# One residual stream instead of two in a list-scheduled transformer kernel: pre-norm gains applied to the transposed stream

## The chip, the cores and the metric

One core of one Trainium2 chip. The metric is the device time of one execution in microseconds. The profile is one execution on the chip, taken by the hardware profiler. TensorE is PE in the rows (PEld its weight loads), VectorE is DVE, ScalarE is ACT, GpSimd is POOL, and SyncE, which issues the loads, is SP.

## What is computed

A decoder of two blocks of two layers each, on one sequence of 256 tokens, 1024 wide, in fp32. Every stage has the same frame: a root-mean-square norm with a pre-gain goes in, the stage's own work is done, and the result is normed with a post-gain and added to the residual stream `x`:

```python
def rms_norm(x, g):
    y = x * lax.rsqrt(jnp.mean(x * x, axis=-1, keepdims=True) + EPS)
    return y * g

for l in range(2):                       # first block
    y = swiglu(rms_norm(x, ffn1_pre_g[l]), ...);        x = x + 0.5 * rms_norm(y, ffn1_post_g[l])
    y = hybrid_mixer(rms_norm(x, mix_pre_g[l]), ...);   x = x + rms_norm(y, mix_post_g[l])
    y = memory_xattn(rms_norm(x, xa_pre_g[l]), ...);    x = x + rms_norm(y, xa_post_g[l])
    y = swiglu(rms_norm(x, ffn2_pre_g[l]), ...);        x = x + 0.5 * rms_norm(y, ffn2_post_g[l])
for l in range(2):                       # second block
    h = rms_norm(x, g_pre_mix[l]);  mix = concat(pool_mixer, dsa_attention of h @ w_in[l]) @ w_out[l]
    x = x + rms_norm(mix, g_post_mix[l])
    h = rms_norm(x, g_pre_ffn[l]);  f = square(relu(h @ w_ff1[l])) @ w_ff2[l]
    x = x + rms_norm(f, g_post_ffn[l])
```

That makes twelve stages: feed-forward, mix, cross-attention, feed-forward, twice over; then mix2 and relu2, twice over. Between them lie eleven hand-overs, each for two row tiles.

## The kernel before

**Tiles.** The 256 tokens are two row tiles `t` = 0, 1 of 128 rows. Tokens lie along the partitions in `x[t]` (128x1024; `x_4` and `x_5` in the order, `x` in the trace). Every fp32 operand of the large products is split into a high part, rounded to fp32r, and the rest, and `mm3` (L518) makes one product of three matmuls: low by high, high by low, high by high. A projection needs the stream with its 1024 features along the partitions: `xT[t]`, a pair of 128x8x128 tiles (high and low), eight slices of 128 features. `xmm` (L523) goes through the eight slices, three matmuls each. Weights come by DMA into `raw`, and `split` (L492) makes `wH` (a copy on ACT) and `wL` (a subtraction on DVE).

**The norm.** The scale `rstd` of a row is left out of the transposed stream and applied when a finished projection is taken out of PSUM, as `scale=rstd[t]` of an ACT instruction (`m<-mm,sm`, `s<-mm,sm`, `nat<-mm,sm` in the trace). `rms_scale` (L531) makes it from a sum of squares: a small DVE instruction, then a power on POOL. The sum of squares of `x` is one ACT instruction, `junkx<-x`.

**The hand-over.** Two streams are kept: `x`, and `xg` = `x` times the next stage's pre-gain. `prepare` (L628) runs earlier in the stage: it broadcasts the post-gain `gp` and the next pre-gain `gg` to 128 partitions, makes `xg[t] = x[t]*gg` and `gg = gg*gp`. `boundary` (L642) runs when the stage's result `acc` (two PSUM tiles of 512 columns for a row tile) is finished:

1. `rms_two` (L544) makes the scale `r` of the post-norm: a sum of squares of each `acc` half on ACT (`junk<-acc`), and a power on POOL.
2. `yg = acc*gg` and `xg += yg*r` on DVE, a half at a time.
3. `transpose_in` (L558) transposes `xg` on PE, four 128x128 transposes into one PSUM tile `tr` (of which there are two), and splits each `tr` with one 512 wide copy on ACT and one 512 wide subtraction on DVE into `xT`.
4. Marked as background: `yp = acc*r` on ACT (`m<-acc,sm`), `yp *= gp` and `x += yp` on DVE, a half at a time.
5. `rstd[t]` of the next stage from the sum of squares of `x[t]`.

**At the start** `start_stream` (L592) loads the first pre-gain as 8x128, transposes it on PE to `gT` (128x8, so that a partition holds its features' gains), and `begin` multiplies the transposed `x` by it, 512 columns in one DVE instruction, before the split.

**What sets the order.** Nothing is issued where it is written. `Recorder.add` (L220) records each operation with the operations it depends on; `plan` (L430) is a list scheduler with a modelled cost for each instruction: PE and SP keep the order of the program, the other engines take what is ready by a deadline (background work yields), and the best of six passes is emitted. So each engine has one fixed order of instructions, and all of them carry the line of `emit`, L449. Two rules of the recorder matter: engines that touch the same PSUM tile are ordered against each other even if both only read (the term `b.psum and o.eng != eng` in `add`), and SP may run 250 PE operations ahead. Buffers (L474): eight `m2` of 512 columns, thirteen `m4` of 1024, four `xT`, and in PSUM four `acc`, two `mm`, two `tr`.

## Time and profile before

| what | value |
|---|---|
| three runs | median 1919.25 us (1919.09 to 1920.76) |
| the profiled execution | 1919.18 us, its span 1917.3 us |
| PE busy | 1886.3 us, 98% of the span |
| DVE busy | 1289.2 us, 67% |
| ACT busy | 1064.1 us, 55% |
| POOL busy | 67.6 us, 4% |
| DMA | 337.55 MB, 176 GB/s |

The span is the time between the first and the last instruction of the profile. A busy share is the time in which an engine executed something, over the span. In a timeline the number in brackets is the time that the engine stood idle before the instruction, and the name behind the arrow is what released it. Buffer numbers are left out of the names: `m` stands for all `m2` and `m4` tiles, `sm` for small columns of one or two numbers (`r` and `rstd` among them), `s` and `nat` for working tiles.

The hand-overs lie here (us from the start of the span): feed-forward to mix at 199 to 210 and 847 to 858; mix to cross-attention at 375 to 381 and 1024 to 1030; cross-attention to feed-forward at 460 to 467 and 1110 to 1117; feed-forward to feed-forward, between the layers, at 652 to 676; feed-forward to mix2 at 1302 to 1320; mix2 to relu2 at 1417 to 1437 and 1720 to 1740; relu2 to mix2 at 1604 to 1622.

### The profile page before, as it was taken

The page shows a single profiled execution, that of the slowest core. Times are in us where ns is not written, and L with a number is a line of the kernel's source. Part 1 is how long each engine was busy: PE and PEld are TensorE (multiplying, and loading weights), DVE is VectorE, ACT ScalarE, POOL GpSimd, SP SyncE. Part 2 cuts the span into 40 slices and gives each one's busy share as a digit, 9 for nine tenths or more (in the row PEclk, how much of TensorE's full clock was granted, in tenths as well). Part 3 has the DMA queues.
Part 4 walks back from the last instruction along what each step waited for, and adds up shares of the span by engine and source line. Part 5 has one row for each costly group of instructions (what it writes and reads, how often), then busy time and mean ns, then how long its engine had stood idle before and what let it go on. Part 6 is the DMA issues. An engine that isn't in the chain of part 4 may idle for free.

```text
span 1917.3 us, 25346 instructions
## 1 busy us (share of the span) xinstructions
PE 1886.3 (98%) x9109; PEld 1536.7 (80%) x9109; DVE 1289.2 (67%) x2172; ACT 1064.1 (55%) x1721; POOL 67.6 (4%) x82
## 2 busy tenths in 40 slices
PE   9999999999999999999999999999999999999998
PEld 7888788888788778878788878888778888777887
DVE  6555888866654764568978675558976557976554
ACT  5444776556444644467656554447664446565443
POOL 0000100100000000010010000000000000000000
PEclk9999999999999999999999999999999999999999
DMA  8555654554655565648354465555446555535553
GB/s 265 179 184 181 202 174 138 176 176 154 202 180 190 164 199 187 194 142 262 113 192 149 144 211 178 184 165 185 141 136 216 186 178 160 176 121 195 178 176 110
DMA packets 230958, 337.55 MB, mean 176 GB/s; under 512 B 17768, under 2 KB 123696, under 8 KB 230832
## 3 DMA queue, kind: packets, MB, share of 16 engines
q1 hardware_dynamic: 230832, 335.92, 54.6%
q8 instruction: 72, 1.18, 0.2%
q14 instruction: 54, 0.44, 0.1%
HBM read 334.82 MB, written 1.05 MB: 175 GB/s over the span
## 4 chain that ended last, share of the span: by engine, by line
PE 81%; DVE 7%; ACT 4%; DMA 3%; issue 3%; POOL 1%; SPq 0%; DVEq 0%; POOLq 0%; ACTq 0%
PE mm L449 46%; PE acc L449 30%; PE tr L449 5%; DVE m L449 2%; ACT wH L449 2%; DVE wL L449 1%; POOL sm L449 1%; ACT m L449 1%; DMA raw<-in_xa_wk_dram 1%; DVE x L449 1%; DMA raw<-in_ffn_w_up_dram 1%; DVE xT L449 1%; DVE xg L449 1%; DMA m<-in_ffn_pre_g_dram 0%; DVE sm L449 0%
## 5 line engine op out<-in xcount | busy, mean ns | idle before, releaser
L449 DVE TENSOR_TENSOR wL<-raw,wH 128x1024 fp32r<-128x1024 f32 (+3 forms) x612 | 731.1, 1200 | 294.2 <-ACT wH L449 285.5
L449 PE MATMUL mm<-wH,xT 128*128 128x512 f32 (+2 forms) x2880 | 912.9, 391 | 7.5 <-ACT m L449 3.7
L449 ACT ACTIVATE wH<-raw 128x1024 fp32r<-128x1024 f32 (+3 forms) x612 | 634.6, 1040 | 313.4 <-PE mm L449 151.3
L449 PEld LDWEIGHTS mm<-wH,xT 128*128 128x128 f32 x2880 | 535.8, 188 | 124.3 <-ACT m L449 4.6
L449 PE MATMUL mm<-wL,xT 128*128 128x512 f32 (+2 forms) x1440 | 565.2, 393 | 0.5 <-DVE wL L449 0.5
L449 PE MATMUL acc<-wH,m 128*128 128x512 f32 (+1 forms) x1408 | 452.1, 393 | 0.5 <-DVE m L449 0.5
L449 PEld LDWEIGHTS mm<-wL,xT 128*128 128x128 f32 x1440 | 271.1, 188 | 56.2 <-DVE wL L449 2.5
L449 PEld LDWEIGHTS acc<-wH,m 128*128 128x128 f32 (+1 forms) x1408 | 258.1, 186 | 55.9 <-DVE m L449 1.3
L449 PE MATMUL acc<-wL,m 128*128 128x512 f32 (+1 forms) x736 | 281.5, 386 | 0.0
L449 PEld LDWEIGHTS acc<-wL,m 128*128 128x128 f32 (+1 forms) x736 | 134.9, 183 | 29.0
L449 ACT ACTIVATE s<-mm,sm 128x256 f32<-128x256 f32 x88 | 41.7, 474 | 188.3 <-PE mm L449 179.8
L449 DVE SCALAR_TENSOR_TENSOR s<-mm,sm,s 128x256 f32<-128x256 f32 x88 | 42.3, 481 | 137.9 <-ACT s L449 137.9
L449 ACT ACTIVATE m<-tr 128x256 fp32r<-128x256 f32 (+5 forms) x208 | 87.6, 426 | 58.7 <-PE tr L449 51.1
L449 POOL TENSOR_TENSOR sm<-sm,neghalf 128x1 f32<-128x1 f32 (+1 forms) x60 | 53.6, 894 | 1842.6 <-ACT sm L449 1665.3
L449 DVE TENSOR_TENSOR m<-tr,m 128x256 fp32r<-128x256 f32 (+3 forms) x192 | 93.1, 495 | 7.3 <-ACT m L449 5.7
L449 PE MATMUL mm<-wH,m 128*128 128x512 f32 x256 | 89.2, 409 | 0.0
L449 PE MATMUL acc<-wH,xT 128*128 128x512 f32 x256 | 82.4, 398 | 0.0
L449 DVE TENSOR_TENSOR m<-acc,m 128x512 f32<-128x512 f32 (+1 forms) x64 | 39.6, 621 | 60.3 <-ACT junk L449 59.4
L449 ACT ACTIVATE nat<-mm,sm 128x512 f32<-128x512 f32 x56 | 38.5, 687 | 70.9 <-PE mm L449 63.4
L449 ACT ACTIVATE junk<-acc 128x512 bf16<-128x512 f32 x48 | 28.5, 593 | 67.9 <-PE acc L449 67.7
L449 PEld LDWEIGHTS acc<-wH,xT 128*128 128x128 f32 x256 | 48.2, 188 | 10.5
L449 ACT ACTIVATE sc<-sc,sm 128x128 f32<-128x128 f32 (+1 forms) x96 | 42.8, 447 | 22.7 <-DVE sm L449 22.0
(152 smaller groups left out, 1469.6 us busy)
## 6 DMA issues: line engine op xcount, KB each, us to landing
raw<-in_w_ff_dram SPq DMA_DIRECT2D x128, 512.0 KB, 4.2
raw<-in_ffn_w_gate_dram SPq DMA_DIRECT2D x176, 256.0 KB, 3.3
raw<-in_ffn_w_up_dram SPq DMA_DIRECT2D x176, 256.0 KB, 3.8
raw<-in_ffn_w_down_dram SPq DMA_DIRECT2D x88, 512.0 KB, 5.0
raw<-in_w_in_dram SPq DMA_DIRECT2D x80, 512.0 KB, 3.8
raw<-in_w_out_dram SPq DMA_DIRECT2D x32, 512.0 KB, 4.1
raw<-in_cmp_w_dram SPq DMA_DIRECT2D x16, 512.0 KB, 4.7
raw<-in_xa_wk_dram SPq DMA_DIRECT2D x16, 512.0 KB, 5.3
```

The source lines that it names most:

```text
L449: getattr(getattr(self.nc, op.eng), op.name)(*[r(v) for v in op.args], **{k: r(v) for k, v in op.kw.items()})
```

## The change

The stream `xg` goes. `prepare` loads the next pre-gain as eight rows of 128 (`load_gT`, 4 KB) and PE transposes it to `gT` (`turn_gT`); the post-gain is scaled by `c` only where `c` is not 1. `boundary` makes `yp = acc*gp` and `x += yp*r` directly, a half at a time, transposes `x`, and the gain is applied as `tr` is split: `transpose_in` with `gT` goes through the four 128 wide pieces of a `tr`, and for each one ACT makes `xh = tr*gT` with the gain as a scale by partition, and DVE makes `tr*gT - xh`. Where a row tile had two copies and two subtractions 512 wide, it now has eight and eight 128 wide. The background part is gone, and `rstd[t]` comes from `x[t]` as before. `begin` uses the same code.

```diff
--- before.py
+++ after.py
@@ -555,7 +555,20 @@
 
         return Lazy(lambda t: (T("xT", [128, 8, 128], F32R), T("xT", [128, 8, 128], F32R)))
 
-    def transpose_in(xt, src, k0=0, nk=8):
+    def load_gT(vec):
+
+        g8 = T("g8", [8, 128], bufs=2)
+        SP.dma_start(g8, vec.rearrange("(k p) -> k p", p=128))
+        return g8
+
+    def turn_gT(g8):
+        tr = P("tr")
+        PE.transpose(tr[:, :8], g8, ident[:8, :8])
+        gT = T("gT", [128, 8], bufs=2)
+        DVE.tensor_copy(gT, tr[:, :8])
+        return gT
+
+    def transpose_in(xt, src, k0=0, nk=8, gT=None):
 
         for b in range(0, nk, 4):
             m = min(4, nk - b)
@@ -563,11 +576,17 @@
             for k in range(m):
                 PE.transpose(tr[:, k * 128:k * 128 + 128], src[:, (b + k) * 128:(b + k) * 128 + 128], ident)
             ks = slice(k0 + b, k0 + b + m)
+            if gT is not None:
+                for k in range(m):
+                    xh, v, g = xt[0][:, k0 + b + k, :], tr[:, k * 128:k * 128 + 128], gT[:, b + k:b + k + 1]
+                    ACT.activation(xh, v, AF.Copy, scale=g)
+                    DVE.scalar_tensor_tensor(xt[1][:, k0 + b + k, :], v, g, xh.bitcast(F32),
+                                             op0=ALU.mult, op1=ALU.subtract)
+                continue
             split(xt[0][:, ks, :], xt[1][:, ks, :], tr[:, :m * 128].rearrange("p (k n) -> p k n", n=128))
 
 
     x = [T(f"x{t}", [128, D]) for t in range(2)]
-    xg = [T(f"xg{t}", [128, D]) for t in range(2)]
     xr = a["x"].rearrange("o (t p) d -> (o t) p d", p=128)
 
     def load_x(t, b):
@@ -591,15 +610,11 @@
 
     def start_stream(pre):
 
-        g8 = T("g8", [8, 128])
-        SP.dma_start(g8, pre.rearrange("(k p) -> k p", p=128))
+        g8 = load_gT(pre)
         SP.dma_start(ident, cst[:, _C_ID:_C_ID + 128])
         load_x(0, 0)
         ACT.activation(small(1), eps, AF.Silu)
-        tr = P("tr")
-        PE.transpose(tr[:, :8], g8, ident[:8, :8])
-        gT = T("gT", [128, 8])
-        DVE.tensor_copy(gT, tr[:, :8])
+        gT = turn_gT(g8)
         xT = new_xT()
         z = T("nat", [128, 128])
         DVE.memset(z, 0.0)
@@ -611,15 +626,7 @@
             for b in range(2):
                 if t or b:
                     load_x(t, b)
-                tr = P("tr")
-                for k in range(4):
-                    c = b * 512 + k * 128
-                    PE.transpose(tr[:, k * 128:k * 128 + 128], x[t][:, c:c + 128], ident)
-                ks = slice(b * 4, b * 4 + 4)
-                n = T("nat", [128, 4, 128])
-                DVE.tensor_tensor(n, tr.rearrange("p (k n) -> p k n", n=128),
-                                  gT[:, ks].unsqueeze(2).to_broadcast([128, 4, 128]), op=ALU.mult)
-                split(xT[t][0][:, ks, :], xT[t][1][:, ks, :], n)
+                transpose_in(xT[t], x[t][:, b * 512:b * 512 + 512], 4 * b, 4, gT[:, 4 * b:4 * b + 4])
             if t == 0:
                 for i in range(3):
                     PE.matmul(warm[:, :128], x[t][:, :128], z, start=True, stop=True)
@@ -629,46 +636,25 @@
 
         gp = T("m4", [128, D])
         bcast_load(gp, post)
-        DVE.tensor_scalar(gp, gp, c, None, op0=ALU.mult)
-        if pre_next is None:
-            return gp, None
-        gg = T("m4", [128, D])
-        bcast_load(gg, pre_next)
-        for t in range(2):
-            DVE.tensor_tensor(xg[t], x[t], gg, op=ALU.mult)
-        DVE.tensor_tensor(gg, gg, gp, op=ALU.mult)
-        return gp, gg
+        if c != 1.0:
+            DVE.tensor_scalar(gp, gp, c, None, op0=ALU.mult)
+        return gp, None if pre_next is None else turn_gT(load_gT(pre_next))
 
     def boundary(t, acc, gains, xT_next):
 
-        gp, gg = gains
-        last = gg is None
+        gp, gT = gains
         r = rms_two(acc[0], acc[1], 512, D)
-        if not last:
-            yg = T("m4", [128, D])
-            for h in range(2):
-                sl = slice(h * 512, h * 512 + 512)
-                DVE.tensor_tensor(yg[:, sl], acc[h], gg[:, sl], op=ALU.mult)
-                DVE.scalar_tensor_tensor(xg[t][:, sl], yg[:, sl], r, xg[t][:, sl], op0=ALU.mult, op1=ALU.add)
-            transpose_in(xT_next[t], xg[t])
-        yp = T("m4", [128, D])
-        halves = [slice(h * 512, h * 512 + 512) for h in range(2)]
-        if last:
-            for h, sl in enumerate(halves):
-                DVE.tensor_tensor(yp[:, sl], acc[h], gp[:, sl], op=ALU.mult)
-            for c in range(0, D, 512):
-                sl = slice(c, c + 512)
-                DVE.scalar_tensor_tensor(x[t][:, sl], yp[:, sl], r, x[t][:, sl], op0=ALU.mult, op1=ALU.add)
+        for h in range(2):
+            sl = slice(h * 512, h * 512 + 512)
+            yp = T("m2", [128, 512])
+            DVE.tensor_tensor(yp, acc[h], gp[:, sl], op=ALU.mult)
+            DVE.scalar_tensor_tensor(x[t][:, sl], yp, r, x[t][:, sl], op0=ALU.mult, op1=ALU.add)
+            if gT is None:
                 SP.dma_start(out.rearrange("o (t p) d -> (o t) p d", p=128)[t][:, sl], x[t][:, sl])
-            return
-        rec.background = True
-        for h, sl in enumerate(halves):
-            evict(yp[:, sl], acc[h], r)
-        for sl in halves:
-            DVE.tensor_tensor(yp[:, sl], yp[:, sl], gp[:, sl], op=ALU.mult)
-            DVE.tensor_tensor(x[t][:, sl], x[t][:, sl], yp[:, sl], op=ALU.add)
-        rec.background = False
-        rstd[t] = rms_scale(sumsq(x[t], D), D)
+            else:
+                transpose_in(xT_next[t], x[t][:, sl], 4 * h, 4, gT[:, 4 * h:4 * h + 4])
+        if gT is not None:
+            rstd[t] = rms_scale(sumsq(x[t], D), D)
 
 
     def ffn_like(nch, load_up, up, load_down, nk, gains, xT, xTn, begin=None):
```

The first place is DVE at the first hand-over from cross-attention to feed-forward (around 464 us in the trace of before). Before, `acc_4294` and `acc_4384` are row tile 1's result, `xg_7` and `x_5` its streams, `xg_6` and `x_4` those of row tile 0; `xT_4435` belongs to row tile 0:

```order
L449 TENSOR_TENSOR m_1022_4367<-acc_4294,m_961_4090 128x512
L449 TENSOR_TENSOR m_1005_4305<-acc_4343,m_961_4090 128x512
L449 SCALAR_TENSOR_TENSOR xg_6_321<-m_1005_4305,sm_4397,xg_6_321 128x512 x2
L449 TENSOR_TENSOR wL_4417<-raw_4325,wH_4400 128x1024
L449 TENSOR_TENSOR xT_4435<-tr_4415,xT_4425 128x512
L449 TENSOR_TENSOR xT_4435<-tr_4423,xT_4425 128x512
L449 TENSOR_TENSOR wL_4447<-raw_4338,wH_4413 128x1024
L449 TENSOR_TENSOR m_1022_4367<-acc_4384,m_961_4090 128x512
L449 SCALAR_TENSOR_TENSOR xg_7_354<-m_1022_4367,sm_4469,xg_7_354 128x512 x2
L449 TENSOR_TENSOR m_1010_4407<-m_1010_4407,m_960_4086 128x512 x2
L449 TENSOR_TENSOR x_4_78<-x_4_78,m_1010_4407 128x512 x2
```

Row tile 0's pieces, 512 wide, stand ahead of row tile 1's update of `xg_7`, and the update of the true `x_4` comes last. In the changed kernel, with `x_4` and `x_5` the streams, `tr_4453` and `tr_4463` the two transposed halves of row tile 0, and `sm_4515` the scale `r` of row tile 1:

```order
L449 SCALAR_TENSOR_TENSOR xT_4472<-tr_4453,gT_4246,xT_4461 128x128
L449 TENSOR_TENSOR wL_4477<-raw_4377,wH_4450 128x1024
L449 SCALAR_TENSOR_TENSOR xT_4472<-tr_4453,gT_4246,xT_4461 128x128
L449 SCALAR_TENSOR_TENSOR xT_4472<-tr_4463,gT_4246,xT_4461 128x128
L449 TENSOR_SCALAR sm_4495<-sm_4467 128x1
L449 TENSOR_TENSOR m_1026_4511<-acc_4423,m_958_4127 128x512
L449 SCALAR_TENSOR_TENSOR xT_4472<-tr_4453,gT_4246,xT_4461 128x128
L449 SCALAR_TENSOR_TENSOR x_5_117<-m_1022_4406,sm_4515,x_5_117 128x512
L449 SCALAR_TENSOR_TENSOR xT_4472<-tr_4453,gT_4246,xT_4461 128x128
L449 SCALAR_TENSOR_TENSOR xT_4472<-tr_4463,gT_4246,xT_4461 128x128
L449 SCALAR_TENSOR_TENSOR x_5_117<-m_1026_4511,sm_4515,x_5_117 128x512
L449 SCALAR_TENSOR_TENSOR xT_4472<-tr_4463,gT_4246,xT_4461 128x128
```

Four pieces of row tile 0 stand ahead of the first update of `x_5` and two more between the first and the second; `x_4` was updated before all of these.

The second place is ACT at the same hand-over. Before, `junk_4453` is the sum of squares of row tile 1's second half, `junkx_4511` that of `x` of row tile 0:

```order
L449 ACTIVATE junk_4453,sm_4454<-acc_4384 128x512
L449 ACTIVATE sm_4462<-sm_4454,sm_4363 128x1
L449 ACTIVATE wH_4466<-raw_4369 128x1024
L449 ACTIVATE m_1027_4476<-acc_4294,sm_4469 128x512
L449 ACTIVATE m_1027_4476<-acc_4384,sm_4469 128x512
L449 ACTIVATE xT_4491<-tr_4484 128x512
L449 ACTIVATE xT_4491<-tr_4494 128x512
L449 ACTIVATE junkx_4511,sm_4512<-x_4_78 128x1024
```

Now, with `junkx_4466` the sum of squares of row tile 0's `x` and `junk_4503` that of row tile 1's second half:

```order
L449 ACTIVATE xT_4461<-tr_4453,gT_4246 128x128
L449 ACTIVATE junkx_4466,sm_4467<-x_4_78 128x1024
L449 ACTIVATE xT_4461<-tr_4453,gT_4246 128x128
L449 ACTIVATE xT_4461<-tr_4463,gT_4246 128x128
L449 ACTIVATE wH_4486<-raw_4391 128x1024
L449 ACTIVATE junk_4503,sm_4504<-acc_4423 128x512
L449 ACTIVATE sm_4509<-sm_4504,sm_4402 128x1
L449 ACTIVATE xT_4461<-tr_4453,gT_4246 128x128
L449 ACTIVATE xT_4461<-tr_4463,gT_4246 128x128
L449 ACTIVATE xT_4461<-tr_4453,gT_4246 128x128
L449 ACTIVATE wH_4521<-raw_4408 128x1024
L449 ACTIVATE xT_4461<-tr_4463,gT_4246 128x128
```

The sum of squares of `x_4` has moved ahead of row tile 1's, and the copies of `tr` stand one by one between the weights' `wH`.

The third place is PE in the first feed-forward stage, where `g_145` is the pre-gain of the mix stage that follows:

```order
L449 MATMUL acc_440<-wH_517,m_101_522 128x512
L449 MATMUL acc_440<-wL_528,m_100_510 128x512
L449 MATMUL acc_440<-wH_517,m_100_510 128x512
L449 MATMUL tr_723<-ident_73,g_145_241 128x8
L449 MATMUL mm_725<-wH_665,xT_113 128x512
L449 MATMUL mm_725<-wL_673,xT_107 128x512
L449 MATMUL mm_725<-wH_665,xT_107 128x512
```

The transpose `tr_723` is new; it stands alone between matmuls 512 wide. Five of the eleven new transposes stand so, and six next to transposes or matmuls of 256 columns or fewer.

## Rows read from the trace of the kernel before

**Rows 1.** The page, part 1: busy time, share of the span, instructions.

```profile
PE 1886.3 (98%) x9109; PEld 1536.7 (80%) x9109; DVE 1289.2 (67%) x2172; ACT 1064.1 (55%) x1721; POOL 67.6 (4%) x82
```

**Rows 2.** Busy time by stretch: us, busy (count) per engine, PEclk, DMA share, GB/s.

```profile
720.00:780.00 60.00, 60.00 (x267) 48.46 (x266) 30.27 (x34) 26.14 (x33) 0.00 (x0) 1.00 0.60 193
...
1305.00:1315.00 10.00, 7.58 (x54) 6.84 (x53) 9.54 (x17) 7.47 (x15) 1.10 (x2) 1.00 0.31 89
...
sum 171.00, PE 159.21 PEld 129.59 DVE 146.04 ACT 113.89 POOL 31.69; mean PE 9.37 PEld 7.62 DVE 8.59 ACT 6.70 POOL 1.86
```

**Rows 3.** Timeline 203 to 211 and one PE row at 1309.94: start, duration [idle<-releaser].

```profile
204.03 1.28 DVE L449 TENSOR_TENSOR x<-x,m 128x512 f32<-128x512 f32 x2
...
205.34 1.06 ACT L449 ACTIVATE junkx<-x 128x1024 bf16<-128x1024 f32 x1 [0.65 <-DVE x L449]
...
207.31 2.19 POOL L449 TENSOR_TENSOR sm<-sm,neghalf 128x1 f32<-128x1 f32 x1 [2.80 <-DVE sm L449]
...
209.54 0.69 ACT L449 ACTIVATE m<-mm,sm 128x512 f32<-128x512 f32 x1 [0.46 <-POOL sm L449]
...
210.28 0.55 PE L449 MATMUL tr<-ident,m 128*128 128x128 f32 x3 [1.07 <-ACT m L449]
...
1309.94 1.29 PE L449 MATMUL tr<-ident,xg 128*128 128x128 f32 x8 [1.14 <-DVE xg L449]
```

**Rows 4.** Groups by line and form: busy us, mean ns, idle before.

```profile
L449 DVE TENSOR_TENSOR m<-m,m 128x512 f32<-128x512 f32 x48 | 31.4, 683 | 0.1
...
L449 ACT ACTIVATE m<-acc,sm 128x512 f32<-128x512 f32 x44 | 28.5, 675 | 0.1
...
L449 DVE TENSOR_TENSOR x<-x,m 128x512 f32<-128x512 f32 x44 | 28.2, 682 | 0.0
...
L449 DVE TENSOR_TENSOR xg<-x,m 128x1024 f32<-128x1024 f32 x22 | 26.3, 1216 | 1.0 <-DMA m<-in_ffn_pre_g_dram 1.0
```

**Rows 5.** Timeline 463 to 467, first hand-over from cross-attention to feed-forward.

```profile
463.64 0.39 PE L449 MATMUL mm<-wH,xT 128*128 128x512 f32 x1
...
463.84 0.60 ACT L449 ACTIVATE junk<-acc 128x512 bf16<-128x512 f32 x1
463.87 0.39 PE L449 MATMUL mm<-wL,xT 128*128 128x512 f32 x1
...
464.56 0.69 DVE L449 TENSOR_TENSOR m<-acc,m 128x512 f32<-128x512 f32 x1 [0.23 <-ACT junk L449]
...
464.93 0.55 POOL L449 TENSOR_TENSOR sm<-sm,neghalf 128x1 f32<-128x1 f32 x1 [5.83 <-ACT sm L449]
...
465.51 1.42 DVE L449 SCALAR_TENSOR_TENSOR xg<-m,sm,xg 128x512 f32<-128x512 f32 x2 [0.27 <-POOL sm L449]
```

**Rows 6.** Timeline of the start, PE.

```profile
17.71 0.50 PE L449 MATMUL mm<-wH,xT 128*128 128x512 f32 x1 [0.57 <-DVE xT L449]
```

**Rows 7.** Timeline 225 to 227, PE, around a lone narrow transpose.

```profile
225.14 0.40 PE L449 MATMUL mm<-wL,xT 128*128 128x512 f32 x1
225.46 0.23 PE L449 MATMUL tr<-ident,pe 16*128 16x16 f32 x1
225.62 0.73 PE L449 MATMUL mm<-wH,xT 128*128 128x512 f32 x2
226.19 0.40 PE L449 MATMUL mm<-wL,xT 128*128 128x512 f32 x1
```

**Rows 8.** Groups by line and form, the shapes nearest to the new pieces.

```profile
L449 ACT ACTIVATE m<-tr 64x128 fp32r<-64x128 f32 x32 | 8.0, 269 | 3.8 <-DVE m L449 3.6
...
L449 DVE SCALAR_TENSOR_TENSOR s<-sc,sm,s 128x128 f32<-128x128 f32 x14 | 4.9, 350 | 0.3
...
L449 ACT ACTIVATE nat<-mm,scl 128x256 f32<-128x256 f32 x8 | 3.6, 470 | 0.4 <-PE mm L449 0.4
```

**Rows 9.** Timeline 1305 to 1306, PE, blocks 292 wide.

```profile
1305.44 0.29 PE L449 MATMUL mm<-wH,xT 128*128 128x292 f32 x1
1305.57 0.29 PE L449 MATMUL mm<-wL,xT 128*128 128x292 f32 x1
```

## The prediction

> **What bounds the kernel now.** I read the page's busy times first, then busy time by stretches of the span, then the waits of TensorE in order of time, and last the costs by shape. TensorE (PE) is busy 98% of the span [rows 1]. In the long feed-forward stretches it is busy all the time, with VectorE (DVE) at half load (the stretch 720 to 780 in [rows 2]), so nothing that DVE or ScalarE (ACT) is spared there can shorten the program, and everything that PE is given there lengthens it. What is left to win lies where one stage hands over to the next. I laid 13 stretches around the handovers in which PE waited, and 4 around handovers in which it did not (mix to cross-attention, both layers): PE is busy 159.21 of 171.00 us in them (the sum in [rows 2]), so the handovers hold 11.8 us of idle PE. The worst is the one into the first mix2 stage, 2.4 us (1305 to 1315 in [rows 2]).
>
> What these waits are made of shows in the first one [rows 3]. The two additions into `x` (row tile 0) run on DVE until 205.31, its sum of squares follows on ACT, the power on POOL lasts from 207.31 to 209.50, and only then can ACT scale the finished projection by `rstd` (209.54); PE, which needs that result for its next transposes, has stood for 1.07 us. So the wait is for `rstd`, and `rstd` is late because the true `x` is updated in the background, after `xg`. Most of the others read alike (a scaled copy or a SiLU that waits for POOL); in the one into mix2 PE also waits 1.14 us for `xg` itself [rows 3].
>
> **The change part by part.** *Work taken off DVE and ACT.* Gone are 22 products `xg = x*gg`, 44 of the 48 products with `gp` in SBUF, 44 additions into `x` and 44 scaled copies on ACT: 26.3 + 28.8 + 28.2 us of DVE and 28.5 of ACT [rows 4]; the eleven `gg*gp` and eight scalings by 1.0 go too. I price all this at nothing by itself: PE covers it. It counts only through what it lets happen earlier.
>
> *`rstd` comes earlier.* In the new program `x` is complete right after the two updates that follow `r`, 1.42 us for the pair (the last of [rows 5]). Two products and two additions leave the chain to `rstd`, 2.7 us at 0.68 each [rows 4], with the scaled copies and all that stood between them, and in the new order the sum of squares of row tile 0 stands ahead of row tile 1's on ACT. No single wait is as long as that. I take all 11.8 us as freed (bounds 0 and 11.8). At the start, PE's 0.57 us wait for a whole split half [rows 6] goes as well, since the first piece now suffices: 0.6 us.
>
> *Eleven more transposes on PE.* Every `turn_gT` puts an 8x128 transpose into PE's queue. The nearest row is the lone transpose of `pe`, 16 partitions: from the matmul before it to the second start after it are 1.05 us, where three matmuls at 0.23 take 0.69, so it costs 0.36; its own slot is 0.16 [rows 5, 7]. In the new order five of the eleven stand alone between wide matmuls and six next to other narrow work, where I charge the slot only: 5 x 0.36 + 6 x 0.16 = 2.7 us, all of it on the bound (bounds 11 x 0.16 = 1.8 and 11 x 0.36 = 3.9). Its load is 4 KB in place of 512 KB on SP's queue, and stands at least 50 PE rows, over 10 us, before the transpose: nothing.
>
> *The split into eight pieces.* This is the part that costs. Before, a half of the transposed tile (512 wide) was one copy on ACT and one subtraction on DVE. Now each 128 wide piece is a scaled copy on ACT and a subtraction on DVE. They read the same PSUM tile, and the program lets two engines read one PSUM tile only in turn: before, DVE's product with `acc` already waited for ACT's sum of squares of the same `acc` (464.56 in [rows 5]). So within a tile ACT's piece 2 waits for DVE's piece 1. A lap is one ACT piece, one DVE piece and two hand-overs. No row has the ACT piece: 128 wide without a pointer takes 0.27, 256 wide with one 0.47 [rows 8]; I take 0.36, the middle. DVE's piece, the same instruction at the same width with its source in SBUF, is 0.35 [rows 8]; I take that. A hand-over is 0.05 (ACT ends at 210.23, PE starts at 210.28 [rows 3]). Lap: 0.81 us. PE eats a piece in three matmuls: 0.70 us where the stage's blocks are 512 wide [rows 5], 0.40 where they are 292 wide [rows 9]. At the nine handovers of the first kind a tile of four pieces falls behind by four times 0.11, so 0.4 us each, 3.6 in all. At the two into mix2 the pieces of the two tiles alternate, and the first tile's come every 0.81 where PE wants them every 0.40: three times 0.41, so 1.2 each, 2.4 in all. Together 6.0 us of new waits. Below this is bounded by 0 (the pieces have enough of a lead), above by 12 (both row tiles pay). I take the middle, since row tile 0 has weight splits between its pieces but a lead of some 3 us, and row tile 1 has no lead.
>
> The Trainium skill speaks against such pieces: "Perfetto Trace Analysis", section "Optimizing Scalar/DVE Operations", gives each instruction on PSUM a fixed part of about 125 ns on DVE and 51 ns on ACT and advises larger operations; but it calls these engine-busy times, adds that the profiled latency is about twice as long, and says that smaller instructions can finish work sooner where the engines are not full. By the busy figures alone a lap would fit under 0.70, the 6.0 would be 0 and the sum 1909.5; a lap is made of latencies, so by the rows it is 6.0.
>
> *Moved to another pool.* `yp` is now two 512 wide `m2` buffers instead of one `m4`. There are eight, and the order gives each its place; nothing.
>
> *The sum.* -11.8 - 0.6 + 2.7 + 6.0 = -3.7 us. The profiled execution took 1919.18 us (span 1917.3 and 1.9 around it), the median of three is 1919.25: the same. So 1919.2 - 3.7 = **1915.5 us**, 0.19% less. About 0.2%, 3.8 us, is what a measurement of this kernel can tell from no change, so this forecast lies on that bound.
>
> **The rivals.** *A, no new waits.* If ACT and DVE keep the pieces ahead of PE, the 6.0 us fall away: 1919.2 - 9.7 = 1909.5. For it: DVE loses 83 us of work [rows 4] just where it is 95% busy (1305 to 1315 in [rows 2]), and the order starts row tile 0's pieces during row tile 1's last matmuls. Against it: ACT, 75% busy there, loses 28.5 us and gets 176 pieces of 0.36 in place of 44 halves.
>
> *B, slower: a piece stuck behind row tile 1's update.* DVE takes its instructions in order. Row tile 1's update of `x` waits for `r`, and pieces of row tile 0 stand behind it. Whoever waits for such a piece pays the power, 0.55, and the update, half of 1.42 and a hand-over [rows 5], 1.3 us together. At all eleven handovers that is 14.3 in place of 6.0, so 1915.5 + 8.3 = 1923.8. It decides where PE needs a piece before `r` exists, some 1.9 us after the last `acc` matmul (463.64 to 465.51 in [rows 5]), which is when PE has used up not quite three pieces. Against it: at nine of the handovers six or more pieces stand ahead of the update, in feed-forward to feed-forward five; only at the first cross-attention to feed-forward, four.
>
> *C, the waits do not go.* If PE's waits are not for `rstd` but for the latency of scaled copy, SiLU and transposes behind a finished projection, an earlier `rstd` changes nothing: 1919.2 + 2.7 = 1921.9. For it: of the 1.07 us in [rows 3], ACT's own wait for POOL is only 0.46. Against it: the projection had been finished meanwhile, and the wait for `xg` has nothing to do with that latency.
>
> **How the numbers follow.** Forecast 0.43, split evenly by the bound (0.21 faster, 0.22 no change); A 0.31; B 0.14; C 0.12. Faster by over 0.2%: 0.52. Within 0.2%: 0.22 + 0.12 = 0.34. Slower: 0.14. The range goes from A with the cheapest transposes (1919.2 - 11.8 - 0.6 + 1.8 = 1908.6) to just under B: 1908.5 to 1923.0. The forecast's own range is 1911 to 1920.
>
> **What would show each step.** Right: in the new profile no wait of PE at 210 or 858 for an ACT result that waited for POOL; the power for row tile 0's `rstd` ending before the projection does; the transposes of `g` at 0.15 to 0.36 us; ACT pieces of 0.36 and DVE pieces of 0.35, each ACT piece starting after a DVE piece; PE idle at the handovers around 6 us instead of 11.8, named "DVE xT". Wrong: PE waits for "DVE x" (B), waits that are still for POOL (C), none at all (A), or idle PE moved into the middle of the mix stages by the new order, which I price at nothing and cannot bound from these rows.

## The result and the profile after

The changed kernel takes 1904.57 us (median of five, 1903.64 to 1905.04); the kernel before, run beside it, 1920.76 (1919.09 to 1921.73). The ratio is 0.9918, with a 95% interval of 0.9906 to 0.993: 0.8% or 16 us faster, where 3.7 us were forecast, and below the stated range. The profiled execution has a span of 1902.6 us against 1917.3.

The busy times of the page, first part, against [rows 1]:

```profile
PE 1883.4 (99%) x9120; PEld 1538.4 (81%) x9120; DVE 1216.3 (64%) x2194; ACT 1065.1 (56%) x1821; POOL 55.4 (3%) x82
```

PE's busy time fell by 2.9 us although eleven transposes came in. In the next fence, groups by line and form (as [rows 4]), they and the new pieces have their durations:

```profile
L449 DVE SCALAR_TENSOR_TENSOR xT<-tr,gT,xT 128x128 fp32r<-128x128 f32 x192 | 62.7, 346 | 22.5 <-ACT xT L449 20.5
...
L449 ACT ACTIVATE xT<-tr,gT 128x128 fp32r<-128x128 f32 x192 | 65.3, 364 | 18.4 <-DVE xT L449 13.6 <-PE tr L449 4.2
...
L449 PE MATMUL tr<-ident,g 8*128 8x8 f32 x12 | 2.7, 228 | 0.0
```

The twelve transposes of `g` (one of them was there before) take 228 ns each, so 2.5 us were added and yet 2.9 went: some 5.4 us of what [rows 1] calls busy was no work. PE's weight loads, PEld, grew by 1.7 us meanwhile. The pieces are what the prediction took: 364 ns on ACT (0.36) and 346 on DVE (0.35).

Busy time by stretch, at the same places as the 17 stretches behind [rows 2], each moved to where its hand-over now lies: the one between the layers, the one into the first mix2 stage, and the sum.

```profile
664.12:675.12 11.00, 10.80 (x49) 8.21 (x48) 6.96 (x13) 5.11 (x9) 1.98 (x1) 1.00 0.84 266
...
1295.30:1305.30 10.00, 9.72 (x62) 8.20 (x61) 8.27 (x22) 8.81 (x26) 1.10 (x2) 1.00 0.45 150
...
sum 171.00, PE 169.62 PEld 138.93 DVE 135.16 ACT 126.97 POOL 13.09; mean PE 9.98 PEld 8.17 DVE 7.95 ACT 7.47 POOL 0.77
```

PE is busy 169.62 of 171 us, against 159.21: of 11.8 us of idle PE, 1.4 are left. That is 10.4 us, less than the kernel gained. The stretch between the layers, in the kernel before, is a row that the prediction did not quote:

```profile
666.00:677.00 11.00, 9.19 (x38) 6.16 (x37) 8.34 (x13) 5.22 (x8) 1.51 (x1) 1.00 0.93 284
```

PE lacks 1.8 us in it, DVE and ACT are not full, and the DMA engines are at 0.93.

Where the time was gained can be read matmul by matmul. The transposes of `g` aside, PE runs the same 9108 instructions in the kernel before and in the changed one, in nearly the same order (of what the plan has ready, PE takes the first in the program's order, so neighbours can change places), so each has its twin in the other trace (good to some 0.3 us). The kernel before falls behind by 15.0 us in all. Between the layers (640 to 690 in the changed kernel) it loses 3.6, at the two hand-overs from feed-forward to mix 1.5 each, at the second from cross-attention to feed-forward 1.1, at the two from mix2 to relu2 1.0 each, at the second into mix2 1.4 and at the first 0.4, at each of the others 0.3 or less, and inside the stages some 3 together. So the most was gained where [rows 2] shows no row, and not at the first hand-over into mix2, which the prediction called the worst.

The timeline of the first hand-over, to be read against [rows 3]:

```profile
201.83 0.55 POOL L449 TENSOR_TENSOR sm<-sm,neghalf 128x1 f32<-128x1 f32 x1 [4.38 <-DVE sm L449]
201.84 0.40 PE L449 MATMUL acc<-wH,m 128*128 128x512 f32 x1
...
206.87 1.05 ACT L449 ACTIVATE junkx<-x 128x1024 bf16<-128x1024 f32 x1
...
208.73 0.69 ACT L449 ACTIVATE m<-mm,sm 128x512 f32<-128x512 f32 x1 [0.20 <-PE mm L449]
```

The power for row tile 0's `rstd` ends at 202.38, half a microsecond after the last `acc` matmul (201.84) has started, where it ended at 209.50 before. So ACT's scaled copy at 208.73 waits for PE's projection and no longer for POOL. Measured so at all eleven hand-overs, from the start of the last `acc` matmul to the end of the power, `rstd` of row tile 0 is ready after 0.4 us in the mean (8.0 before) and that of row tile 1 after 9.6 (14.6 before). The power itself is part of this: it took 2.19 us in [rows 3] and 0.55 here, in the mean over the eleven 1.14 before and 0.55 now, for row tile 1 1.30 and 0.76. Of these 44 powers in the two traces, each that took over 0.6 us ran beside a DVE instruction with all its operands in SBUF (`wL<-raw,wH`, `m<-m,m`, `xg<-m,sm,xg`); the others ran beside instructions that read PSUM, such as the pieces, or beside none, but for overlaps of at most 0.11 us. No run was made to show why.

What PE waited for in the whole program, from the view of waits (us, times, longest), before:

```profile
PE mm L449 <- ACT m L449: 3.7, 4, 1.2
...
PE tr L449 <- ACT m L449: 2.2, 2, 1.1
PE tr L449 <- DVE s L449: 2.0, 4, 0.5
...
PE tr L449 <- DVE xg L449: 1.3, 2, 1.1
```

and after:

```profile
PE tr L449 <- DVE m L449: 2.0, 5, 0.5
PE tr L449 <- DVE nat L449: 1.9, 2, 1.1
...
PE mm L449 <- DVE xT L449: 0.8, 3, 0.4
```

Gone are the waits for ACT's scaled copies (`m`) and for `xg`, and those for `s` fell from 2.0 to 0.3. In their place stand 0.8 us of waits for pieces, "DVE xT". The waits for DVE's `m` and `nat` stood in the middle of the stages before as well (1.8 and 2.6). But all these are only the waits that the rows show as idle. The timeline of the first mix2 stage:

```profile
1302.80 0.63 ACT L449 ACTIVATE xT<-tr,gT 128x128 fp32r<-128x128 f32 x2 [0.16 <-DVE xT L449]
...
1303.19 0.81 PE L449 MATMUL mm<-wH,xT 128*128 128x292 f32 x2
1303.20 0.61 DVE L449 SCALAR_TENSOR_TENSOR xT<-tr,gT,xT 128x128 fp32r<-128x128 f32 x2 [0.18 <-ACT xT L449]
...
1303.58 0.37 ACT L449 ACTIVATE xT<-tr,gT 128x128 fp32r<-128x128 f32 x1 [0.16 <-DVE xT L449]
1303.60 0.19 PEld L449 LDWEIGHTS mm<-wH,xT 128*128 128x128 f32 x1 [0.35 <-DVE xT L449]
...
1303.98 0.35 DVE L449 SCALAR_TENSOR_TENSOR xT<-tr,gT,xT 128x128 fp32r<-128x128 f32 x1 [0.18 <-ACT xT L449]
...
1304.43 0.36 ACT L449 ACTIVATE xT<-tr,gT 128x128 fp32r<-128x128 f32 x1
...
1304.76 0.43 PE L449 MATMUL mm<-wH,xT 128*128 128x292 f32 x2
```

Two `tr` tiles take turns: a row with x2 holds a piece of each. ACT's next piece of a tile waits for DVE's last one, and a lap takes 0.78 us (1302.80 to 1303.58; 0.81 was forecast). PE's pair of 292 wide matmuls takes 0.81 here, and 0.43 where nothing is late (1304.76). The second of the pair waits for its weight load, which waited for the piece, and the row counts the wait as busy.

### The profile page after: what moved, and what is told of

Read it like the earlier page. It is cut to its first block, busy times and chain, and to the rows that moved or that the text cites. A ratio compares the mean times of both kernels' runs of the same rounds, so it can differ in the third digit from the quotient of the medians.

```text
span 1902.6 us, 25467 instructions
## 1 busy us (share of the span) xinstructions
PE 1883.4 (99%) x9120; PEld 1538.4 (81%) x9120; DVE 1216.3 (64%) x2194; ACT 1065.1 (56%) x1821; POOL 55.4 (3%) x82
## 4 chain that ended last, share of the span: by engine, by line
PE 88%; DVE 6%; ACT 2%; DMA 2%; issue 1%; POOL 0%; SPq 0%; DVEq 0%; POOLq 0%; ACTq 0%
PE mm L449 51%; PE acc L449 31%; PE tr L449 5%; DVE wL L449 2%; DVE m L449 1%; ACT wH L449 1%; DVE sc L449 1%; DVE sm L449 1%; DVE xT L449 1%; DMA raw<-in_xa_wk_dram 1%; DMA raw<-in_w_in_dram 1%; ACT xT L449 0%; DVE s L449 0%; POOL sm L449 0%; ACT junkx L449 0%
## 5 line engine op out<-in xcount | busy, mean ns | idle before, releaser
L449 POOL TENSOR_TENSOR sm<-sm,neghalf 128x1 f32<-128x1 f32 (+1 forms) x60 | 41.3, 689 | 1839.2 <-ACT sm L449 1664.0
L449 DVE SCALAR_TENSOR_TENSOR xT<-tr,gT,xT 128x128 fp32r<-128x128 f32 x192 | 62.7, 346 | 22.5 <-ACT xT L449 20.5
L449 ACT ACTIVATE xT<-tr,gT 128x128 fp32r<-128x128 f32 x192 | 65.3, 364 | 18.4 <-DVE xT L449 13.6
```

What stands on the lines that cost most here:

```text
L449: getattr(getattr(self.nc, op.eng), op.name)(*[r(v) for v in op.args], **{k: r(v) for k, v in op.kw.items()})
```

## The experiments

Differences below are between medians, those of the changed kernel (1904.57) and of before (1920.76) as above. Beside the experiments the kernel before had medians from 1920.41 to 1922.21, and each interval of a ratio against it is about 0.0025 wide (4.8 us), so a difference from before is certain to some 2.4 us and one between two of the other kernels to some 3. Part of the scatter is TensorE's granted clock, the mean over a run: it was 0.998 or 0.999 in the runs of the changed kernel, 0.999 to 1.0 in those of e4, e5 and e10, and 0.994 to 0.998 in those of e6 and e16. Within one kernel, 0.001 less goes with some 1.2 us more (an estimate, a line through all runs).

| kernel | median us | to the changed kernel | `rstd` ready, row tiles 0 and 1 |
|---|---|---|---|
| before | 1920.76 | +16.2 | 8.0, 14.6 |
| changed | 1904.57 | 0 | 0.4, 9.6 |
| e1 halves | 1915.0 | +10.4 | 6.5, 10.8 |
| e2 two streams, short chain | 1928.24 | +23.7 | 8.1, 14.5 |
| e3 late, with work | 1939.89 | +35.3 | 8.5, 18.2 |
| e4 same work, not late | 1904.53 | 0.0 | 4.2, 9.4 |
| e5 no transposes of g | 1900.56 | -4.0 | 0.4, 9.4 |
| e6 four for one | 1931.15 | +26.6 | 0.4, 9.6 |
| e7 changed, new plan | 1903.94 | -0.6 | 0.4, 9.5 |
| e8 before, new plan | 1920.73 | +16.2 | 8.0, 14.6 |
| e9 two streams, pieces | 1928.53 | +24.0 | 7.7, 16.1 |
| e10 halves, no gain | 1899.72 | -4.9 | 1.2, 7.5 |
| e11 loads back | 1909.08 | +4.5 | 0.4, 9.5 |
| e12 late, no work | 1912.58 | +8.0 | 8.3, 10.6 |
| e13 all of prepare back | 1912.52 | +8.0 | 0.4, 9.5 |
| e14 prepare and late | 1923.47 | +18.9 | 8.3, 10.6 |
| e15 gain in the weights | 1911.28 | +6.7 | 2.9, 7.8 |
| e16 prepare, both late | 1931.74 | +27.2 | 10.9, 14.5 |

Three theories stood at the start: 1, `x` and `rstd` are ready earlier; 2, DVE and ACT have less to do; 3, the pieces let PE start sooner.

**A new plan alone (e7, e8).** Every edit makes the scheduler plan anew, so its luck comes first. Edit of both:

```diff
-    LAT = 110.0
+    LAT = 116.0
```

> The changed kernel with one number of the scheduler's model moved, the latency between engines from 110 to 116, so that every engine's order is planned anew with no change of work. It shows how far a new order alone moves the time. If the stalls in the middle of the stages are the order's luck: 2 to 4 us either way from the changed kernel. If not: within 1 us.

> The kernel before with the same number moved from 110 to 116. If the order's luck moves the time: 2 to 4 us either way from before, and part of the measured gain could be luck. If not: within 1 us.

Neither median moved by more than 0.6 us; by the ratios to the kernel before beside them, 0.9907 and 0.9996, the moves are 2.1 and 0.8, inside the intervals. The orders did change: 160 of DVE's 2194 instructions stand elsewhere in e7, and 145 of 2172 in e8. So much luck lies in the order in two trials; a difference above some 3 us between two kernels here is hardly the order's luck.

**The pieces (e1, e10, e9).** e1 puts the halves back with a product on DVE. e10 puts them back without one: it leaves the pre-gains out of the eleven hand-overs and the start, so it computes something else and serves only to time the halves. e9 brings the pieces into the kernel before.

```diff
# e1, in transpose_in
-                for k in range(m):
...
+                n = T("nat", [128, 4, 128])
+                DVE.tensor_tensor(n, tr.rearrange("p (k n) -> p k n", n=128),
+                                  gT[:, b:b + m].unsqueeze(2).to_broadcast([128, 4, 128]), op=ALU.mult)
+                split(xt[0][:, ks, :], xt[1][:, ks, :], n)
# e10
+                split(xt[0][:, ks, :], xt[1][:, ks, :], tr[:, :m * 128].rearrange("p (k n) -> p k n", n=128))
# e9, before, for xg
+                for k in range(m):
+                    split(xt[0][:, k0 + b + k, :], xt[1][:, k0 + b + k, :], tr[:, k * 128:k * 128 + 128])
```

> One stream as in the change, but the gain is applied to a whole 512 wide half at once (one DVE product into SBUF, then one copy and one subtraction), so the 128 wide pieces are undone. Theory 1 (the gain comes from x and rstd being ready earlier): the waits at the hand-overs stay away, 11 to 15 us below the kernel before; a little is lost, because a half needs three instructions of 0.6 to 0.7 us before PE may start. Theory 2 (the gain comes from DVE and ACT having less to do): DVE gets 44 products of about 0.6 us back, a third of the 83 us that it lost, so about a third of the gain goes, 9 to 11 us below before. Theory 3 (the gain comes from the small pieces, since PE starts after the first quarter of a half): most of the gain goes, at most 5 us below before.

> The changed kernel with the gain left out of the stream altogether, so that each transposed half is one 512 wide copy and one 512 wide subtraction as before the change; the pre-gains are loaded and transposed and then not applied. One stream, no extra product: e1_halves without its 44 products on DVE. If e1 lost its 10 us through whole halves: again 1911 to 1915 us. If e1 lost them through its added products, which push rstd back to 6.5 us: within 2 us of the changed kernel, 1903 to 1907 us, with rstd of row tile 0 back at 1 to 4 us.

> The kernel before with one edit: the transposed xg is split in 128 wide pieces (plain copies and subtractions, eight and eight) instead of 512 wide halves. Two streams stay, and rstd of row tile 0 stays at about 8 us after the last acc matmul. If the pieces themselves carry the gain (PE starts after the first quarter): 7 to 12 us below before. If rstd's lateness carries it: 0 to 3 us below. By the prediction's term, pieces cost 6 us: 3 to 6 us above before.

After e1 it looked as if the pieces carried the gain; e10 overthrew that. Whole halves without the product are 4.9 us faster than pieces, so pieces cost about 5 us, and on the kernel before they cost 7.8 (e9). e1 lost its time through its products, 44 at the hand-overs of 0.68 us each, which stand on DVE in the chain to the next stage: e1 against e10 is 15.3 us, and `rstd` of row tile 0 is back at 6.5. The price does not show as idle PE: with the same 9120 PE instructions the profiled execution of e10 is 3.7 us shorter than that of the changed kernel (1898.9 against 1902.6), and PE's busy time is 3.8 us less (1879.6 against 1883.4). Twin by twin, some 3.4 us of this lie at the two hand-overs into mix2 (3.0 at the first) and 1.0 at the other nine together, 0.8 of that at the first cross-attention to feed-forward; over the rest of the program 0.9 comes back. In the first mix2 stage of e10, with two instructions for eight, PE is busy throughout:

```profile
1295.00:1305.00 10.00, 10.00 (x71) 9.48 (x70) 7.75 (x13) 7.80 (x17) 1.99 (x3) 1.00 0.70 234
```

**Lateness (e12, e3, e4).** e12 makes `rstd` of row tile 0 late by one tiny instruction. e3 and e4 put the old background chain back, e3 into the chain to `rstd` and e4 beside it.

```diff
# e12, in boundary
-            rstd[t] = rms_scale(sumsq(x[t], D), D)
+            s = sumsq(x[t], D)
+            if t == 0:
+                rstd[0] = s
+            else:
+                v = small(1)
+                DVE.scalar_tensor_tensor(v, xT_next[1][1][:, 3, 0:1].bitcast(F32), 0.0, rstd[0],
+                                         op0=ALU.mult, op1=ALU.add)
+                rstd[0], rstd[1] = rms_scale(v, D), rms_scale(s, D)
# e3; in e4 the last line reads sumsq(x[t], D)
+            for h, sl in enumerate(halves):
+                evict(z[:, sl], acc[h], r)
+            for sl in halves:
+                DVE.tensor_tensor(z[:, sl], z[:, sl], gp[:, sl], op=ALU.mult)
+                DVE.scalar_tensor_tensor(z[:, sl], z[:, sl], 0.0, x[t][:, sl], op0=ALU.mult, op1=ALU.add)
+            rstd[t] = rms_scale(sumsq(z, D), D)
```

> The changed kernel with rstd of row tile 0 made late without any work worth the name: one DVE instruction on 128x1 adds zero times a number of row tile 1's fourth transposed piece to its sum of squares, so that rstd of row tile 0 waits for that piece, about 8 to 9 us after the last acc matmul, as in the kernel before (8.0) instead of 0.4. The pieces stay. If lateness of rstd carries the gain: 8 to 12 us above the changed kernel, 1912 to 1917 us. If the pieces carry it: 0 to 3 us above it. Both in part: 4 to 7 us.

> The changed kernel with the old background chain put back between the update of x and rstd: two scaled copies of acc on ACT, two products and two instructions on DVE that put x into another buffer, and the sum of squares is taken of that. So rstd is as late as before and DVE and ACT have about the old work, while x, its transposes and the pieces are as in the change. Theory 1: the waits for rstd come back, 3 to 7 us below before. Theory 2: the same. Theory 3: the gain stays, 12 to 15 us below. Its partner e4 tells 1 and 2 apart.

> As e3_late, the same added instructions, but rstd is taken from x itself and waits for none of them; their result is used by nothing. Theory 1: rstd is as early as in the change, 11 to 15 us below before. Theory 2: the work is back, so the waits are back, 3 to 7 us below, as in e3_late. Theory 3: 12 to 15 us below.

e12 costs 8.0 us with no work (`rstd` of row tile 1 comes 1.0 later too). Twin by twin, hardly any of it arises before the second cross-attention to feed-forward; that hand-over and the four that follow lose 1.2 to 2.6 us each (at the two into mix2 the granted clock of this execution also fell to half for a while, from 1306.36 and from 1610.15). Its timeline in the first mix2 stage shows the chain, the tiny instruction, the power, and the scaled copy that waits for it:

```profile
1306.05 0.16 DVE L449 SCALAR_TENSOR_TENSOR sm<-xT,sm 128x1 f32<-128x1 f32 x1
...
1306.54 0.55 POOL L449 TENSOR_TENSOR sm<-sm,neghalf 128x1 f32<-128x1 f32 x1 [2.66 <-DVE sm L449]
...
1307.13 0.50 ACT L449 ACTIVATE m<-mm,sm 128x292 f32<-128x292 f32 x1 [0.66 <-POOL sm L449]
```

e3 and e4 run the same instructions, but for what the sum of squares reads: 35.3 us where `rstd` waits for them (that of row tile 1 then comes later than in the kernel before), 0.0 where nobody does, or some 1 us by e4's higher clock. So not the load on DVE and ACT counts but who waits for it. e4 also shows how early is early enough: `rstd` at 4.2 us costs nothing, since the first projection, 24 matmuls at 0.23 [rows 5], is finished only after some 5.5 us.

**A short chain beside `xg` (e2).**

```diff
-        rec.background = True
-        for h, sl in enumerate(halves):
-            evict(yp[:, sl], acc[h], r)
-        for sl in halves:
-            DVE.tensor_tensor(yp[:, sl], yp[:, sl], gp[:, sl], op=ALU.mult)
-            DVE.tensor_tensor(x[t][:, sl], x[t][:, sl], yp[:, sl], op=ALU.add)
+        for h, sl in enumerate(halves):
+            DVE.tensor_tensor(yp[:, sl], acc[h], gp[:, sl], op=ALU.mult)
+            DVE.scalar_tensor_tensor(x[t][:, sl], yp[:, sl], r, x[t][:, sl], op0=ALU.mult, op1=ALU.add)
```

> The kernel before with one edit: x is updated by two DVE products acc*gp and two multiply-adds, in the foreground, in place of two scaled copies on ACT, two products and two additions in the background. Both streams and the 512 wide halves stay. Theory 1: rstd is earlier, so the waits that end with POOL's power go; the waits for xg into mix2 stay; 6 to 10 us below before. Theory 2: DVE does about the same (four instructions for four, the two on PSUM not shorter) and ACT 28 us less, little changes, 0 to 3 us below. Theory 3: nothing changes, 0 to 1 us.

A miss for all three theories: 7.5 us above before. The edit did not do what it was meant to, `rstd` came no earlier (8.1). It does not bear on lateness. Its view of waits shows where it loses: PE waits 9.4 us for the weight copies `wH` (2.5 before) and 2.6 for `wL` (0.5), so it looks as if the update, no longer in the background, came ahead of the weights' splits; no run was made to show that.

**Loads and products of `prepare` (e11, e13, e14, e16).**

```diff
# e11
+        bcast_load(T("m4", [128, D]), pre_next)
# e13: e11 (into gg), and
+        for t in range(2):
+            DVE.tensor_tensor(z, x[t], gg, op=ALU.mult)
+        DVE.tensor_tensor(gg, gg, gp, op=ALU.mult)
# e14: e13 and e12. e16: e14, and for rstd[1]
+                for i in range(8):
+                    w = small(1)
+                    POOL.tensor_tensor(w, v, one, op=ALU.pow)
+                    v = w
```

> The changed kernel with the eleven broadcast loads of 512 KB put back, into a buffer that nothing reads: the DMA traffic of before and nothing else. If the smaller traffic is behind the small gains in the middle of the stages: 1 to 3 us above the changed kernel. If the loads are covered, as the prediction had it: within 1 us of it.

> The changed kernel with prepare's old work put back: the broadcast load of the next pre-gain, the two products x*gg, the product gg*gp and the scaling of gp by 1.0; their results are used by nothing. The load alone costs 4.5 us (e11). If the products hold the 12 us that are not accounted for: 10 us or more above the changed kernel, 1914 to 1921 us. If they are covered, as the prediction had it: within 2 us of e11, 1907 to 1911 us.

> e13 with the late rstd of e12 as well. If the parts simply add: e13 plus 8 us. If lateness and a loaded DVE cost more together than apart (a wait starts a backlog that the next hand-over's work meets): e13 plus 11 us or more. If they share their waits: e13 plus 5 us or less.

> e14 with rstd of row tile 1 late as well, by a chain of eight powers with exponent 1 on POOL, which is nearly idle: about 4.5 us later, 15 us after the last acc matmul, as in the kernel before (14.6). If that is the rest of the account: 4 to 8 us above e14, 1927 to 1931 us. If not: within 1.5 us of e14.

The loads alone cost 4.5 us. Twin by twin, e11 loses 2.3 us between the layers and 1.7 at the second cross-attention to feed-forward, and 0.3 or less at each of the other nine. The timeline of e11 after the hand-over between the layers:

```profile
671.98 1.06 ACT L449 ACTIVATE wH<-raw 128x1024 fp32r<-128x1024 f32 x1 [3.79 <-DMA raw<-in_ffn_w_up_dram]
...
673.09 0.72 PE L449 MATMUL mm<-wH,xT 128*128 128x512 f32 x2 [1.91 <-ACT wH L449]
```

ACT stands 3.79 us for a weight load, and PE 1.91 for the weights. From 650 to 676 a load of `ffn_w_gate` lands 5.3 us after its issue in the median, and one of `ffn_w_down` after 8.4; in the changed kernel, after 3.7 and 5.8. Over the program PE waits 4.8 us for `wH` in e11 and 1.3 in the changed kernel:

```profile
PE mm L449 <- ACT wH L449: 4.8, 3, 1.9
```

```profile
PE mm L449 <- ACT wH L449: 1.3, 1, 1.3
```

The products on top cost 3.4 (e13), about as much as two medians here can tell apart. A late `rstd` on top of these costs 11 us (e14), not 8, so the parts cost more together; a late `rstd` of row tile 1 another 8.3 (e16). In e16 the longer queue on POOL also made row tile 0's later (10.9), so part of the 8.3 belongs there.

**The transposes of `g` (e5, e6).**

```diff
# e5, in prepare
-        return gp, None if pre_next is None else turn_gT(load_gT(pre_next))
+        gT = T("gT", [128, 8], bufs=2)
+        SP.dma_start(gT, pre_next.rearrange("(k p) -> p k", p=128), allow_slow_non_contiguous=True)
# e6
+        for i in range(4):
+            gT = turn_gT(load_gT(pre_next))
```

> The changed kernel without the eleven transposes of g: each pre-gain is loaded straight into its 128x8 form by a DMA of single numbers; the one at the start stays. By the spacing in the trace a transpose of g costs PE 0.25 us (0.34 in the two mix2 stages), 2.9 us for eleven: 2.5 to 3.3 us below the changed kernel, if the order is otherwise the same. Rival: the transposes sit in PE's slack or their loads delay weights, 0 to 1 us either way; the DMA of 1024 numbers of 4 bytes may hold up a weight load and make it slower.

> The changed kernel with each pre-gain loaded and transposed four times, the last one used: 33 more transposes, copies and loads. At 0.25 to 0.34 us each: 8.2 to 11.2 us above the changed kernel. Where PE has slack for them: under 3 us.

e5 is 4.0 us faster than the changed kernel and, at 0.989 of before (0.9878 to 0.9903), the fastest here that computes the whole reference. In the changed kernel's timeline a lone transpose reads

```profile
526.89 0.39 PE L449 MATMUL acc<-wH,m 128*128 128x512 f32 x1
527.22 0.23 PE L449 MATMUL tr<-ident,g 8*128 8x8 f32 x1
527.37 0.50 PE L449 MATMUL mm<-wH,xT 128*128 128x512 f32 x1
527.71 0.39 PE L449 MATMUL mm<-wL,xT 128*128 128x512 f32 x1
```

so from the matmul before it to the second one behind it are 0.82 us where two at 0.23 would take 0.46: 0.36 each, since the matmul behind it is slower too (0.50 at 527.37, 0.39 at 527.71). Against the same places in e5, up to the third instruction behind, the eleven cost 0.30 to 0.36 each, 3.8 in all; at four of them, in the middle of stages (346, 989, 1385 and 1685), half or more of it is made up three instructions later. Another 0.4 of e5's gain stood there before the first of them: at the start, from 9 to 13, the changed kernel's profiled execution was granted 0.57 of the clock (it fell to 0.50, which is 1.2 GHz, after PE had stood 1.31 us for `wH`) and that of e5 all of it. e6 does not price a transpose: 33 of them cost 26.6 us, 0.81 each, because `g8` has two buffers and the third load waits for the first transposes; near a hand-over PE waits for it:

```profile
440.52 0.37 PE L449 MATMUL tr<-ident,g 8*128 8x8 f32 x2 [3.31 <-DMA g<-in_ffn_pre_g_dram]
```

There are four such long waits in e6: 3.31 and 3.23 for `g`, and two of 2.69 (at 355.83 and 1012.04) for DVE's `m`. Soon behind each the granted clock is at half, 1.2 GHz (0.50 in 442.0 to 445.4), so part of the 26.6 lies there.

**The gain in the weights (e15).** Pieces, transposes and second stream all go; the weights' rows are scaled as they are split.

```diff
+            for k in range(ku):
+                gk = g[:, k0 + k:k0 + k + 1]
+                ACT.activation(H[:, k], raw[:, k], AF.Copy, scale=gk)
+                DVE.scalar_tensor_tensor(L[:, k], raw[:, k], gk, H[:, k].bitcast(F32), op0=ALU.mult, op1=ALU.subtract)
```

> One stream, no pieces, no transposes of g (loaded by a DMA of single numbers): the transposed x is split in 512 wide halves without a gain, and the gain is applied to the rows of the weights as they are split, each weight unit in two 512 wide scaled copies on ACT and two multiply-subtracts on DVE in place of one 1024 wide of each. The pieces cost 4.8 us and the transposes 4.0, so if the dearer weight splits are covered: 1895 to 1898 us. Against it: each unit takes about 0.3 us more on ACT and 0.2 us more on DVE, and at the hand-overs the weights are late already: 1905 to 1915 us.

6.7 us slower than the changed kernel, inside the second range: the dearer splits seem not to be covered. PE waits 3.4 us for `wH` (1.3 in the changed kernel), but also 5.1 for DVE's `m` (2.0) and 2.1 for `xT` (0.8); which of these come from the splits was not separated.

## Why the prediction was wrong

The direction was right, the size was not. The account by the runs, all as differences; the first three lines are e16 taken apart, which stands for the kernel before but has the pieces and the transposes:

- late `rstd` of both row tiles, on top of the rest: 11.0 + 8.3 = 19.3 us (e14 - e13, e16 - e14)
- the broadcast loads: 4.5 us (e11)
- the products of `prepare`: 3.4 us (e13 - e11)
- less the pieces, 4.9 (e10), and the transposes, 4.0 (e5)

27.2 - 8.9 = 18.3 us, where 16.2 were measured; the difference is within the uncertainty of such a sum and of e16, whose granted clock was lower and whose `rstd` of row tile 0 is later than before.

**The step that failed: "I take all 11.8 us as freed (bounds 0 and 11.8)".** The idle PE of 17 stretches stood as the most that could be freed. By this account 25 to 27 us were (16.2 and the 8.9 that was paid, or the sum), against 12.4 with the 0.6 of the start. Three things were missed in it.

First, idle time is not all that a wait costs. Rows in which PE waits for a weight load count as busy, as the pair of 0.81 us and the busy time of e10 show, and some 5.4 us of busy time without work went. What [rows 3] left out at 210.28 is the weight load of the same wait, 1.38 us where PE's row has 1.07:

```profile
210.28 0.31 PEld L449 LDWEIGHTS tr<-ident,m 128*128 128x128 f32 x3 [1.38 <-ACT m L449]
```

The Trainium skill says so of the whole program ("Perfetto Trace Analysis", section "Identifying the Most-Contended Engine"): matmul busy share is no good measure of how close a kernel is to its roofline, and the weight loads' busy share is one to use instead. The traces agree so far: by PE the kernel before was at 98%, by PEld at 80% [rows 1].

Second, the size of the lateness. The prediction counted two products and two additions, 2.7 us, and left "all that stood between them" without a number; `rstd` came 7.6 us earlier for row tile 0 and 5.0 for row tile 1. Row tile 1's was not considered at all. That lateness costs time is shown by e12, with no work, and by e3 against e4; that it is the largest part, 19.3 of 27.2, rests on e14 and e16.

Third, the loads. "4 KB in place of 512 KB on SP's queue ... nothing" looked only at whether the small load is in time. What counted was that the large one was in the way of the weights, in the stretch between the layers, whose DMA share was 0.93, and at one other. That is 4.5 us.

**"I price all this at nothing by itself: PE covers it."** Right for the background chain (e4, 0.0). For the products of `prepare` it is off by up to 3.4 us.

**The pieces, 6.0 us.** Right in total (4.9 by e10), and right in the lap: 0.364 and 0.346 us, 0.78 for 0.81. Where it falls was half right: at the two hand-overs into mix2 some 3.4 us, where 2.4 were forecast, and at the nine others 1.0, where 3.6 were. So the laps that fall behind by 0.11 at 512 wide blocks are not seen, the price at mix2 is higher, and that the total is near is in part luck. By the Trainium skill's busy figures ("Perfetto Trace Analysis", section "Optimizing Scalar/DVE Operations") a lap was estimated to fit under 0.70 us; measured, it took 0.78, and the same section says that latency is about twice the busy time. Its advice to group work into larger operations where the engine is saturated goes with e10: into the first mix2 stage ACT was busy 8.81 and DVE 8.27 of 10 us.

**The transposes, 2.7 us.** 4.0 by e5, some 3.6 behind the start, near the upper bound of 3.9 (and 5 x 0.36 + 6 x 0.16 is 2.8, not 2.7). The 0.36 for one that stands alone was right. The six beside narrow work were charged 0.16 and cost 0.30 to 0.36 up to the third instruction behind, though four of them give half or more of that back.

**The start, 0.6 us.** The wait of [rows 6] fell from 0.57 to 0.20 us (17.48), and another came in: 0.47 us before the transposes of `x` at 19.81. The first hand-over's last `acc` matmul starts at 201.84 instead of 202.12, so 0.3 were gained.

**The rivals.** A gave 1909.5, nearest to the result, but for a reason that does not hold: the pieces do cost. C is refuted by the view of waits, in which those for ACT's `m` are gone, and by e12. A relative of B is seen once, where B was placed, at the first hand-over from cross-attention to feed-forward:

```profile
463.17 0.69 DVE L449 TENSOR_TENSOR m<-acc,m 128x512 f32<-128x512 f32 x1 [0.96 <-ACT junk L449]
...
463.78 0.34 DVE L449 SCALAR_TENSOR_TENSOR xT<-tr,gT,xT 128x128 fp32r<-128x128 f32 x1
...
464.18 0.50 PE L449 MATMUL mm<-wH,xT 128*128 128x512 f32 x1 [0.43 <-DVE xT L449]
```

Row tile 1's product with `acc` stood 0.96 us in DVE's queue waiting for ACT's sum of squares, and row tile 0's next piece came behind it; PE waited 0.43 us, not 1.3. The update that waits for `r`, of which B spoke, came only after that piece.

## What to carry to other kernels

Do not take the idle time of the busiest engine as the most that a change can free: waits hide in its busy rows and in its weight loads, a wide load can hold up the weights where the DMA engines are nearly full (0.93 here), and one late value can cost at several hand-overs. Ask of each removed instruction who waits for it: the same work cost 35 us in the chain to the next stage and nothing beside it. A wide copy of a vector that only the partitions need, 512 KB for 4 KB of numbers, is dear where the next stage's weights are being loaded (two of eleven hand-overs here), and one PE transpose to put it there cost more here than a DMA of single numbers.

## What was not expected of the hardware

The DMA of 1024 single numbers into 128x8 lands after 3.7 to 6.4 us (median 5.7), not much later than weight loads of 256 or 512 KB (medians of 3.5 to 5.4 in e5), and is the cheaper way:

```profile
gT<-in_ffn_pre_g_dram SPq DMA_DIRECT2D x3, 4.0 KB, 3.8
gT<-in_mix_pre_g_dram SPq DMA_DIRECT2D x2, 4.0 KB, 6.1
```

It is not free: twin by twin, e5 loses 1.1 us between the layers and 0.7 at the second cross-attention to feed-forward, the two places where the broadcast loads cost.

The other is how little a second reader of a PSUM tile costs per turn, and how much in sum: DVE starts 0.03 us after ACT's piece has ended (1303.95 to 1303.98), and ACT as soon after DVE's (0.35 after 1303.20, and at 1303.58 again ACT). Yet with two short instructions to a lap PE falls from 0.40 to 0.78 us for three 292 wide matmuls.
